# Three edits in the tail of a float32 decoder layer: where split weights lie, when a head's second products run, and how the last block is folded into the residual

## The chip, the cores and the metric

The kernel runs on one core of one Trainium2 chip. The metric is device time in microseconds (us), from the first to the last instruction with what lies around it, median of three runs. A profiled execution on the chip gives the trace that the rows below come from. Engines: TensorE (PE: matrix products), VectorE (DVE), ScalarE (ACT), GpSimd (POOL) and SyncE (SP), whose queue here issues nearly all transfers.

## The reference, cut to what matters

One decoder layer over 1024 tokens and 1024 channels in float32. Three attention branches give outputs `o_A`, `o_B`, `o_C` (1024 x 512 each); then:

```
# o_n @ P_n: branch n, 512 -> 1024 channels; G_n: its gate
x = x + (sum_n sigmoid(G_n) * (o_n @ P_n)) @ W_o  # merge and output projection
h = rms_norm(x, norm_mlp)
x = x + square(relu(h @ W_up)) @ W_down           # 1024 -> 4096 -> 1024
```

All three edits lie in these lines, the last 900 us of the kernel; attention stands before them and is not touched.

## The kernel before, in words

**Arithmetic.** Every float32 matrix product is done as three products of split parts: an operand is split into a high part `h` (ScalarE copies it to the rounded type, line 90) and a low part `l`, source minus high (line 91, on VectorE or GpSimd), and `mm3` (lines 112 to 117) adds h·h, h·l and l·h into one PSUM bank. So each weight block costs a load on SyncE's queue into a raw tile `wr`, a ScalarE copy and a subtraction. TensorE runs in the written order; the other engines' orders come from a planner that simulates the program with modelled costs and lets whatever is ready first, by program order, go first. Each engine, and each queue of transfers, then works strictly in that order. A tile pool hands a buffer on when its last reader is done.

**Merge (`merge_and_mlp`, lines 1151 to 1197).** Branch A was multiplied earlier. Branch B: eight blocks d by two halves of the tokens (`half`), each a product of 12 matmuls (`branch`) into one of six banks; VectorE multiplies it with the gate `g` (line 1179; gates are loaded through two buffers), GpSimd adds it to `y` (line 1181). Branch C: for each half, eight blocks; VectorE does the gate (1190), the addition (1192) and the low part of the result (1194), ScalarE the high part (1193), giving `mh`, `ml`, the operand of the output projection. The weights' split parts come from `weight` and `parts`: three buffers of each part, in pool `pre`. The pools `bb` (split `ob`), `br` (`y` and `oc` of half 0) lie on the right above `pre`, `bl` (`y`, `oc` of half 1) and `bg` (gates) on the left.

**Output projection (`tail`, lines 1231 to 1309).** The eight k-blocks of W_o are split into `wo`, whose first four lie where `bb` was and last four where `br` was. Each half block is loaded into one of the three raw tiles `wr` of `pre`, which the branches' weights use too, and split, with the subtraction on VectorE for odd k and on GpSimd for even k. Then come eight row tiles of 128 tokens in the order 0, 4, 1, 5, 2, 3, 6, 7: two halves of 24 matmuls into a bank each, added to `x1` (the loaded residual; tag x1, two buffers in pool `xp`, line 1298), stored to `xd`, normed (`norm`) and, one row tile later, transposed on TensorE. From row tiles 4 to 7 `operands` makes sums of blocks as well: `tt`, `rb` on VectorE (lines 1280 to 1288) and the split operands t1, t2, t3, t4.

**MLP.** Both matrix products go by Winograd's form of Strassen's scheme: 2 x 2 blocks, seven products (numbers 1 to 7) instead of eight; products 2, 7 and 3 are added in the banks of 1, 6 and 5 (`chain`), after VectorE or ScalarE has read those. Weights (and, for the down product, the stored activations) are combined in sums `s1` to `s4`, `t1` to `t4` (`sums`, line 1224). *Up stage*: 16 pairs of blocks, products in the order 1, 6, 5, 2, 7, 4, 3 (`ORDER`), 12 matmuls each. The first four pairs (`HEAD`) do products 1 and 2 early, straight from loaded weights, while row tile 7 is being transposed and split: `after(1)` copies product 1's bank to `e1` on ScalarE (line 1366), then product 2 goes on in that bank. Activations are combined and stored to `ud`. *Down stage*: eight batches `b` of two pairs. In each batch seven products in `order`; per product and pair the stored `ud` is loaded into `v` (tag v, four buffers, line 1458) and split with VectorE, the weight is loaded by `raw` (seven raw tiles over two pools, line 1329), summed on GpSimd (line 1224) and split with GpSimd. Four row tiles j of 6 matmuls follow, and VectorE adds each bank to its accumulator (line 1477): products 1, 6, 7 to `sums`, products 2 to 5 to `x1`. In the last batch `sums` are folded into `x1` after products 6 and 7 (line 1481), eight additions on VectorE and twelve on GpSimd, and each finished piece is stored.

Of the kernel before, what the change touches and what calls it, by code (L numbers as in the profile page):

```python
# [11 lines left out]
F32 = mybir.dt.float32  # L12
F32R = mybir.dt.float32r
AF = mybir.ActivationFunctionType
# [3 lines left out]
P = 128  # L18
# [57 lines left out]
class Kernel:  # L76
# [27 lines left out]
    def parts(self, pool=None, bufs=None, tag="w"):  # L104
        return [(pool or self.wp).tile([P, self.w_n], F32R, name=tag + x, tag=tag + x, bufs=bufs or self.w_bufs)
                for x in "hl"]
# [64 lines left out]
    def run(self):  # L171
# [3 lines left out]
        self.spreads = []  # L175
        self.urgent = URGENT
# [974 lines left out]
    def merge_and_mlp(self):  # L1151
# [9 lines left out]
        with (tc.tile_pool(name="bb", side="right", **kw) as bb, tc.tile_pool(name="br", side="right", **kw) as br,  # L1161
              tc.tile_pool(name="bl", side="left", **kw) as bl, tc.tile_pool(name="bg", side="left", **kw) as bg):
# [68 lines left out]
    def tail(self, mp, mh, ml, halves, pre):  # L1231
# [10 lines left out]
        for k in range(KT):  # L1242
            for s in halves:
                r = pre.tile([P, 512], F32, name="wr", tag="wr", bufs=3)
                nc.sync.dma_start(r, a["wo"][k, :, s])
                self.split(wo[k][0][:, s], wo[k][1][:, s], r, nc.vector if k % 2 else nc.gpsimd)
# [4 lines left out]
        def norm(t, x1):  # L1251
# [7 lines left out]
            def operands():  # L1259
# [28 lines left out]
                sub(b21, b21, t2)  # L1288
# [4 lines left out]
        self.first = {}  # L1293
        HEAD = 4
# [23 lines left out]
        last = {}  # L1318
# [95 lines left out]
        for i in range(1, HEAD):  # L1414
# [4 lines left out]
            pairs[i - 1].product(2, 1, True)  # L1419
        pairs[-1].product(2, 1, True)  # L1420
# [4 lines left out]
        for o in pairs:  # L1425
            up(o, [i for i in self.ORDER if i not in (1, 2)])
        for p in range(HEAD, H):
# [8 lines left out]
        into = {2: lambda j: x1[j][:, lo], 3: lambda j: x1[j][:, hi], 4: lambda j: x1[4 + j][:, lo],  # L1436
                5: lambda j: x1[4 + j][:, hi]}
        G = 2
        order = (1, 6, 7, 2, 5, 4, 3)
# [7 lines left out]
        for b in range(0, H, G):  # L1447
# [5 lines left out]
            final = b + G == H  # L1453
            for i in order:
                forms = []
                for q in range(G):
                    u = temp("v")
# [9 lines left out]
                for j in range(4):  # L1467
# [5 lines left out]
                    dst = sums[i][j] if i in sums else into[i](j)  # L1473
                    if i in sums and b == 0:
                        nc.scalar.activation(dst, ps, AF.Copy)
                    else:
                        nc.vector.tensor_tensor(dst, dst, ps, op=ALU.add)
                    if not final:
                        continue

                    add = lambda o, x, eng: eng.tensor_tensor(o, o, x, op=ALU.add)  # L1481
                    if i == 6:
                        add(sums[6][j], sums[1][j], nc.gpsimd)
# [70 lines left out]
```

## Time and profile before

| | us |
|---|---|
| median of 3 runs (lowest, highest) | 2107.08 (2104.51, 2108.21) |
| the profiled execution's own time | 2108.54 |
| its span, first to last instruction | 2106.7 |
| TensorE busy in the span | 1956.2 |
| VectorE, ScalarE, GpSimd busy in the span | 1404.5, 1020.7, 956.9 |

The profiled execution lies 1.46 us above the median of the runs and has 1.84 us around its span. Busy time is an average over stages with different limits, so the tail is read stage by stage. Stages, by TensorE: merge from 1219 us, output projection from 1313.8, up stage from 1427, down stage from 1757.5, end at 2106.7.

### The profile page before, as it was taken

The page shows a single profiled execution, that of the slowest core. Times are in us where ns is not written, and L with a number is a line of the kernel's source. Part 1 is how long each engine was busy: PE and PEld are TensorE (multiplying, and loading weights), DVE is VectorE, ACT ScalarE, POOL GpSimd, SP SyncE. Part 2 cuts the span into 40 slices and gives each one's busy share as a digit, 9 for nine tenths or more (in the row PEclk, how much of TensorE's full clock was granted, in tenths as well). Part 3 has the DMA queues.
Part 4 walks back from the last instruction along what each step waited for, and adds up shares of the span by engine and source line. Part 5 has one row for each costly group of instructions (what it writes and reads, how often), then busy time and mean ns, then how long its engine had stood idle before and what let it go on. Part 6 is the DMA issues. An engine that isn't in the chain of part 4 may idle for free. (4 is left out here: it accounts for less than half of the span.)

```text
span 2106.7 us, 30550 instructions
## 1 busy us (share of the span) xinstructions
PE 1956.2 (93%) x9806; PEld 1613.4 (77%) x9806; DVE 1404.5 (67%) x3207; ACT 1020.7 (48%) x2622; POOL 956.9 (45%) x1149
## 2 busy tenths in 40 slices
PE   6999998998799999999999799898999998999997
PEld 6778777788678778887888677686788886877876
DVE  5747667778848667647776736358645544888877
ACT  5355455566636555536565523324444544433332
POOL 4455345354252212162222145227444445878777
PEclk9999999999999999999999999899999999999998
DMA  6131012011211111202243366424444436444443
GB/s 212 49 101 49 6 54 57 13 49 35 85 27 59 60 47 53 75 28 88 80 129 99 119 224 188 132 85 156 171 143 150 150 137 222 147 144 140 141 134 110
DMA packets 122909, 218.42 MB, mean 104 GB/s; under 512 B 14260, under 2 KB 35252, under 8 KB 122748
## 3 DMA queue, kind: packets, MB, share of 16 engines
q1 hardware_dynamic: 118076, 202.84, 30.0%
q10 hardware_dynamic: 4672, 13.63, 1.8%
q8 instruction: 77, 1.26, 0.3%
q14 instruction: 84, 0.69, 0.1%
HBM read 155.54 MB, written 64.81 MB: 105 GB/s over the span
## 5 line engine op out<-in xcount | busy, mean ns | idle before, releaser
L91 POOL TENSOR_TENSOR wl<-wr,wh 128x512 fp32r<-128x512 f32 (+3 forms) x246 | 320.4, 1309 | 300.5 <-ACT wh L90 242.9
L90 ACT ACTIVATE wh<-wr 128x512 fp32r<-128x512 f32 (+3 forms) x258 | 150.4, 590 | 217.6 <-PE mm L116 130.0
L697 PE MATMUL sc<-st 128*128 128x256 f32 (+5 forms) x736 | 199.3, 352 | 16.0 <-ACT p L729 15.8
L90 ACT ACTIVATE ph<-tr 128x384 fp32r<-128x384 f32 (+3 forms) x280 | 138.3, 496 | 117.0 <-PE tr L745 98.5
L91 DVE TENSOR_TENSOR pl<-tr,ph 128x384 fp32r<-128x384 f32 (+3 forms) x280 | 155.5, 558 | 46.2 <-ACT ph L90 43.0
L742 POOL MEMSET ph<- 128x128 f32 x152 | 34.1, 224 | 304.5 <-PE ac L887 265.2
L697 PEld LDWEIGHTS sc<-st 128*128 128x128 f32 x736 | 124.8, 189 | 56.6 <-ACT p L729 24.3
L116 PE MATMUL mm<-wl,wh 128*128 128x512 f32 x352 | 142.7, 405 | 22.6 <-POOL wl L91 22.6
L115 PE MATMUL mm<-hh,wh 128*128 128x512 f32 x384 | 159.6, 416 | 0.0
L117 PE MATMUL mm<-hh,wl 128*128 128x512 f32 x384 | 152.0, 396 | 0.0
L116 PE MATMUL mm<-hl,wh 128*128 128x512 f32 x384 | 151.9, 396 | 0.0
L745 PE MATMUL tr<-ident,p 128*128 128x128 f32 x792 | 132.2, 280 | 15.4 <-ACT o L875 7.9
L91 DVE TENSOR_TENSOR wl<-v,wh 128x512 fp32r<-128x512 f32 x112 | 132.6, 1188 | 20.7 <-ACT wh L90 16.8
L115 PE MATMUL mm<-wh 128*128 128x512 f32 x352 | 140.8, 400 | 2.8 <-ACT wh L90 2.8
L117 PE MATMUL mm<-wh,wl 128*128 128x512 f32 x352 | 141.1, 401 | 0.0
L729 ACT ACTIVATE p<-sc,mc 128x256 f32<-128x256 f32 (+5 forms) x200 | 106.7, 538 | 52.3 <-DVE mc L721 50.2
L887 PE MATMUL ac<-ph,st 128*128 128x256 f32 x392 | 110.2, 299 | 19.1 <-DVE ob L894 13.0
L115 PE MATMUL mm<-wh,hh 128*128 128x384 f32 (+1 forms) x320 | 125.0, 391 | 0.0
L91 POOL TENSOR_TENSOR wl<-s,wh 128x512 fp32r<-128x512 f32 x64 | 87.0, 1363 | 81.9 <-ACT wh L90 78.8
L115 PE MATMUL mm<-mh,wh 128*128 128x512 f32 x256 | 102.5, 400 | 9.5 <-ACT e L1366 9.2
L888 PE MATMUL ac<-pl,st 128*128 128x256 f32 x392 | 105.8, 291 | 5.7 <-DVE pl L91 4.9
L745 PEld LDWEIGHTS tr<-ident,p 128*128 128x128 f32 x792 | 91.9, 142 | 24.8 <-ACT o L875 10.5
(308 smaller groups left out, 5733.5 us busy)
## 6 DMA issues: line engine op xcount, KB each, us to landing
ud<-u SPq DMA_DIRECT2D x112, 256.0 KB, 2.1
v<-ud SPq DMA_DIRECT2D x112, 256.0 KB, 2.8
wr<-wu SPq DMA_DIRECT2D x72, 256.0 KB, 2.8
wr<-wd SPq DMA_DIRECT2D x64, 256.0 KB, 2.9
gd<-go SPq DMA_DIRECT2D x48, 256.0 KB, 2.0
g<-gd SPq DMA_DIRECT2D x48, 256.0 KB, 3.0
wr<-wg SPq DMA_DIRECT2D x40, 256.0 KB, 2.7
wr<-wbr SPq DMA_DIRECT2D x40, 256.0 KB, 2.8
```

Of the source, the lines that this page charges most:

```text
L90: nc.scalar.activation(hi, src, AF.Copy)
L91: (eng or nc.vector).tensor_tensor(lo, src, hi.bitcast(F32), op=ALU.subtract)
L115: mm(out, lh, rh, start=first, stop=False, skip_group_check=more)
L116: mm(out, lh, rl, start=False, stop=False, skip_group_check=more)
L117: mm(out, ll, rh, start=False, stop=last, skip_group_check=more)
L697: self.nc.tensor.matmul(ps[:, off:off + k1 - k0], q[:, t * P:(t + 1) * P], k[:, k0:k1], start=i == 0, stop=i == 1)
L729: self.nc.scalar.activation(p, ps, AF.Exp, bias=m, scale=-1.0, accum_out=l)
L742: nc.gpsimd.memset(ph[0:rows, o:o + P].bitcast(F32), 0.0)
L745: nc.tensor.transpose(pt[0:rows, o:o + P], src, self.ident)
L887: nc.tensor.matmul(ac, v, ph, start=first, stop=False)
L888: nc.tensor.matmul(ac, v, pl, start=False, stop=last)
```

## The change

- `parts` takes a weight's high and low tile in turn from `pre` and from a new pool `wx` (as many buffers again), from the merge on.
- W_o's blocks are loaded whole (512 KB, one transfer per k) into the two x1 buffers of `xp`, not in halves into the raw tiles of `pre`.
- In the up stage's head, product 2 of the four pairs runs after product 1 of all four; before, it ran one pair behind. The transposes of row tile 7 stay behind pair 1's product 1. What VectorE does for the head pairs' other products is queued behind the last block sum of row tile 7 (`last["sum"]`).
- In the down stage the order is 1, 6, 2, 7, 5, 4, 3; from the second batch on, activations load into the 12 buffers of tag u, which the sums t1 to t4 use too, and no longer into the 4 of tag v.
- In the last batch the accumulators of the earlier batches are folded into `x1` up front, twenty additions on VectorE, and each bank is added straight to the one, two or three pieces of `x1` that it belongs to: 40 additions from banks, where there were 28.

```diff
--- before.py
+++ after.py
@@ -102,8 +102,11 @@
         return hi, lo
 
     def parts(self, pool=None, bufs=None, tag="w"):
-        return [(pool or self.wp).tile([P, self.w_n], F32R, name=tag + x, tag=tag + x, bufs=bufs or self.w_bufs)
-                for x in "hl"]
+        pool = pool or self.wp
+        if self.other is not None:
+            self.turn += 1
+            pool = self.other if self.turn % 2 else pool
+        return [pool.tile([P, self.w_n], F32R, name=tag + x, tag=tag + x, bufs=bufs or self.w_bufs) for x in "hl"]
 
     def spare(self, k):
 
@@ -173,6 +176,7 @@
         PS = bass.MemoryType.PSUM
         self.lag, self.turn = [], 0
         self.spreads = []
+        self.other = None
         self.urgent = URGENT
         self.through = True
         self.dram = tc.alloc_tile_pool(name="dram", bufs=1, space=bass.MemoryType.DRAM)
@@ -1159,7 +1163,9 @@
         self.wp = pre
         self.w_n, self.wr_bufs, self.w_bufs = 512, 3, 3
         with (tc.tile_pool(name="bb", side="right", **kw) as bb, tc.tile_pool(name="br", side="right", **kw) as br,
-              tc.tile_pool(name="bl", side="left", **kw) as bl, tc.tile_pool(name="bg", side="left", **kw) as bg):
+              tc.tile_pool(name="bl", side="left", **kw) as bl, tc.tile_pool(name="bg", side="left", **kw) as bg,
+              tc.tile_pool(name="wx", side="left", **kw) as wx):
+            self.other = wx
             ob = [[bb.tile([P, S], F32R, name=f"ob{i}{x}") for x in range(2)] for i in range(4)]
             oc = [None, None]
             y = [None, None]
@@ -1240,10 +1246,10 @@
         wps = [tc.alloc_tile_pool(name=f"wo{i}", side="right", **kw) for i in range(2)]
         wo = [[wps[k // 4].tile([P, D], F32R, name=f"wo{k}{x}") for x in range(2)] for k in range(KT)]
         for k in range(KT):
+            r = xp.tile([P, D], F32, name="x1", tag="x1", bufs=2)
+            nc.sync.dma_start(r, a["wo"][k])
             for s in halves:
-                r = pre.tile([P, 512], F32, name="wr", tag="wr", bufs=3)
-                nc.sync.dma_start(r, a["wo"][k, :, s])
-                self.split(wo[k][0][:, s], wo[k][1][:, s], r, nc.vector if k % 2 else nc.gpsimd)
+                self.split(wo[k][0][:, s], wo[k][1][:, s], r[:, s], nc.vector if k % 2 else nc.gpsimd)
         g = xp.tile([P, D], F32, name="g2")
         nc.scalar.dma_start(g, a["norm_mlp"].broadcast_to([P, D]))
 
@@ -1285,12 +1291,13 @@
                 self.split(mh[:, 0:4, ts], ml[:, 0:4, ts], wide(t1), nc.gpsimd)
                 sub(b11, t2, b11)
                 self.split(th["t3"][0][:, :, js], th["t3"][1][:, :, js], wide(b11), nc.gpsimd)
-                sub(b21, b21, t2)
+                last["sum"] = nc.vector.tensor_tensor(b21, b21, t2, op=ALU.subtract).ins
                 self.split(th["t4"][0][:, :, js], th["t4"][1][:, :, js], wide(b21))
 
             return operands
 
         self.first = {}
+        last = {}
         HEAD = 4
         late = []
         for t in (0, 4, 1, 5, 2, 3, 6, 7):
@@ -1315,7 +1322,6 @@
             moving[n] = (*th[n], 0, lo)
         main = more = None
         count = dict(f=0, r=0)
-        last = {}
 
         def form():
             count["f"] += 1
@@ -1416,14 +1422,15 @@
             pairs[i].after(1)
             if i == 1:
                 late.pop()()
-            pairs[i - 1].product(2, 1, True)
-        pairs[-1].product(2, 1, True)
+        for o in pairs:
+            o.product(2, 1, True)
         xp.release()
         more = tc.alloc_tile_pool(name="more", side="right", **kw)
         for o in pairs:
             o.after(2)
         for o in pairs:
-            up(o, [i for i in self.ORDER if i not in (1, 2)])
+            with tc.issue_after(last["sum"]):
+                up(o, [i for i in self.ORDER if i not in (1, 2)])
         for p in range(HEAD, H):
             up(up_pair(p), self.ORDER)
         tf.release()
@@ -1433,10 +1440,11 @@
         acc = tc.alloc_tile_pool(name="acc", side="left", **kw)
         x1 = [acc.tile([P, D], F32, name=f"x1{t}") for t in range(NT)]
         sums = {i: [acc.tile([P, 512], F32, name=f"a{i}{j}") for j in range(4)] for i in (1, 6, 7)}
-        into = {2: lambda j: x1[j][:, lo], 3: lambda j: x1[j][:, hi], 4: lambda j: x1[4 + j][:, lo],
-                5: lambda j: x1[4 + j][:, hi]}
+        place = {2: lambda j: (j, lo), 3: lambda j: (j, hi), 4: lambda j: (4 + j, lo), 5: lambda j: (4 + j, hi)}
+        place.update({i: place[5] for i in sums})
+        add = lambda o, x: nc.vector.tensor_tensor(o, o, x, op=ALU.add)
         G = 2
-        order = (1, 6, 7, 2, 5, 4, 3)
+        order = (1, 6, 2, 7, 5, 4, 3)
         banks = 0
 
         def bank():
@@ -1451,10 +1459,17 @@
                 gets.append(self.sums(wd, temp, "t", nc.gpsimd))
             held = {}
             final = b + G == H
+            if final:
+                for j in range(4):
+                    add(sums[6][j], sums[1][j])
+                    add(x1[j][:, hi], sums[6][j])
+                    add(sums[7][j], sums[1][j])
+                    add(x1[4 + j][:, lo], sums[7][j])
+                    add(x1[4 + j][:, hi], sums[7][j])
             for i in order:
                 forms = []
                 for q in range(G):
-                    u = temp("v")
+                    u = temp("u" if b else "v")
                     nc.sync.dma_start(u, ud[b + q][i])
                     forms.append((splitted(u, nc.vector), splitted(gets[q](self.BSIDE[i]), nc.gpsimd)))
                 if b == 0 and i in (1, 6):
@@ -1470,24 +1485,18 @@
                     for q in range(G):
                         (uh, ul), (wh, wl) = forms[q]
                         self.mm3(ps, uh[:, js], ul[:, js], wh, wl, q == 0 and not chain, q == G - 1, bool(chain))
-                    dst = sums[i][j] if i in sums else into[i](j)
-                    if i in sums and b == 0:
-                        nc.scalar.activation(dst, ps, AF.Copy)
-                    else:
-                        nc.vector.tensor_tensor(dst, dst, ps, op=ALU.add)
-                    if not final:
+                    if i in sums and not final:
+                        if b == 0:
+                            nc.scalar.activation(sums[i][j], ps, AF.Copy)
+                        else:
+                            add(sums[i][j], ps)
                         continue
 
-                    add = lambda o, x, eng: eng.tensor_tensor(o, o, x, op=ALU.add)
-                    if i == 6:
-                        add(sums[6][j], sums[1][j], nc.gpsimd)
-                        add(x1[j][:, hi], sums[6][j], nc.gpsimd)
-                    elif i == 7:
-                        add(sums[7][j], sums[1][j], nc.vector)
-                        add(x1[4 + j][:, lo], sums[7][j], nc.gpsimd)
-                        add(x1[4 + j][:, hi], sums[7][j], nc.vector)
-                    if i in into:
-                        t, s = {2: (j, lo), 3: (j, hi), 4: (4 + j, lo), 5: (4 + j, hi)}[i]
+                    t, s = place[i](j)
+                    for t, s in {1: ((j, hi), (4 + j, lo), (4 + j, hi)), 6: ((j, hi),),
+                                 7: ((4 + j, lo), (4 + j, hi))}.get(i, ((t, s),)):
+                        add(x1[t][:, s], ps)
+                    if final and i in (2, 3, 4, 5):
                         nc.sync.dma_start(a["out"][t * P:(t + 1) * P, s], x1[t][:, s])
         acc.release()
         more.release()
```

## Rows read from the trace of the kernel before

**Rows 1.** The profile page's first part: TensorE's busy time over the whole span, its share, its instructions.

```profile
PE 1956.2 (93%) x9806; PEld 1613.4 (77%) x9806; DVE 1404.5 (67%) x3207; ACT 1020.7 (48%) x2622; POOL 956.9 (45%) x1149
```

**Rows 2.** The windows view, one stretch of the tail a line: its length, then busy time (and instructions) of each engine, the granted clock, the DMA share, GB/s. Branch 1; branch 2; the first two row tiles of the output projection; its other six; the head of the up stage; the stretch after it.

```profile
1219.00:1265.60 46.60, 44.52 (x192) 35.91 (x193) 15.46 (x19) 9.26 (x15) 23.09 (x18) 1.00 0.77 257
1265.60:1313.80 48.20, 45.38 (x194) 35.50 (x193) 29.66 (x43) 17.10 (x30) 28.80 (x22) 1.00 0.58 179
1313.80:1355.20 41.40, 31.84 (x99) 20.82 (x98) 17.30 (x24) 12.62 (x21) 11.92 (x10) 0.75 0.49 158
1355.20:1427.00 71.80, 71.80 (x343) 59.57 (x342) 34.26 (x47) 19.82 (x38) 11.16 (x10) 1.00 0.23 85
1427.00:1461.70 34.70, 25.47 (x108) 20.07 (x107) 33.46 (x28) 20.68 (x38) 32.75 (x20) 0.90 0.44 147
1461.70:1520.00 58.30, 54.72 (x232) 42.88 (x231) 38.64 (x47) 25.47 (x42) 27.29 (x21) 1.00 0.52 180
```

**Rows 3.** The waits view of TensorE from 1150 us on: engine and line, whom it waited for, us in total, times, the longest.

```profile
PE mm L116 <- POOL wl L91: 22.6, 12, 4.2
PE mm L115 <- ACT e L1366: 9.2, 2, 7.6
```

**Rows 4.** The timeline of SyncE's queue around the output weights: start, length, queue, line, transfer.

```profile
1304.40 0.33 SPq L1245 DMA_DIRECT2D wr<-wo  x1
...
1318.52 14.87 SPq L1245 DMA_DIRECT2D wr<-wo  x10
```

**Rows 5.** The tile view of wo: an engine's instructions on it with their shortest, median and longest ns, first and last start; the last line is the time from issue to landing of its transfers.

```profile
L90 ACT ACTIVATE wo<-wr x16: 613/630/635, 1308.1 to 1335.7; 128x512 fp32r<-128x512 f32 x16
L91 POOL TENSOR_TENSOR wo<-wr,wo x8: 1267/1284/1787, 1308.8 to 1333.2; 128x512 fp32r<-128x512 f32 x8
DMA to landing us min/median/max: 2.5/2.9/3.7
```

**Rows 6.** The timeline of VectorE in the merge: the last lower parts of half 0 and the last of half 1.

```profile
1301.90 1.29 DVE L1194 SCALAR_TENSOR_TENSOR ml<-y,mh 128x512 fp32r<-128x512 f32 x2
...
1323.75 0.69 DVE L1194 SCALAR_TENSOR_TENSOR ml<-y,mh 128x512 fp32r<-128x512 f32 x1
```

**Rows 7.** The lines view of VectorE in the merge, 1219 to 1325 us: group and count, busy us, mean ns, idle before it and what ended it.

```profile
L1179 DVE SCALAR_TENSOR_TENSOR g<-g,mm 128x512 f32<-128x512 f32 x16 | 10.9, 685 | 32.0 <-DMA g<-gd 26.7 <-PE mm L117 5.1
```

**Rows 8.** The source view of L1299, the loads of the residual rows x1 (512 KB each): the time from issue to landing.

```profile
DMA to landing us min/median/max: 3.4/3.4/10.9
```

**Rows 9.** The timeline of ScalarE in the head: the copies e of pairs 2 and 3, and two splits between them.

```profile
1446.05 0.58 ACT L1366 ACTIVATE e<-mm 128x512 f32<-128x512 f32 x1
...
1453.92 1.15 ACT L90 ACTIVATE wh<-s 128x512 fp32r<-128x512 f32 x2 [4.40 <-DVE s L1224]
...
1456.71 0.58 ACT L1366 ACTIVATE e<-mm 128x512 f32<-128x512 f32 x1
```

**Rows 10.** The timeline of VectorE in the head: the first and the last of the eleven sums s of the head pairs before 1461.7 us.

```profile
1436.19 1.20 DVE L1224 TENSOR_TENSOR s<-wr 128x512 f32<-128x512 f32 x1
...
1460.54 1.77 DVE L1224 TENSOR_TENSOR s<-wr 128x512 f32<-128x512 f32 x1
```

**Rows 11.** The windows view of the down stage, one batch of two pairs a line (third, fourth, fifth, seventh and eighth), and last a stretch across the seventh and eighth.

```profile
1846.20:1885.20 39.00, 38.43 (x170) 31.47 (x169) 33.06 (x42) 14.80 (x27) 27.67 (x20) 1.00 0.43 138
1885.20:1927.80 42.60, 39.80 (x170) 32.51 (x169) 34.48 (x42) 16.19 (x30) 34.02 (x24) 0.96 0.44 128
1927.80:1967.50 39.70, 38.68 (x170) 31.39 (x169) 32.55 (x42) 15.38 (x29) 34.16 (x24) 1.00 0.51 162
2006.50:2051.50 45.00, 40.81 (x170) 33.24 (x169) 34.12 (x42) 15.01 (x28) 31.67 (x23) 0.92 0.42 135
2051.50:2103.70 52.20, 43.55 (x169) 34.28 (x167) 43.09 (x47) 11.84 (x21) 43.65 (x29) 0.90 0.31 107
2035.20:2090.10 54.90, 48.53 (x194) 39.06 (x193) 48.02 (x53) 17.79 (x32) 51.11 (x34) 0.91 0.29 92
```

**Rows 12.** The waits view of SyncE's queue in the down stage.

```profile
SPq L1458 <- DVE wl L91: 142.7, 61, 7.7
SPq L1329 <- POOL wl L91: 68.6, 36, 5.0
```

**Rows 13.** The timeline of GpSimd at the start of the seventh batch: a sum u, then the split wl that TensorE waits for.

```profile
2008.31 1.72 POOL L1224 TENSOR_TENSOR u<-wr,u 128x512 f32<-128x512 f32 x1
2010.00 1.70 POOL L91 TENSOR_TENSOR wl<-wr,wh 128x512 fp32r<-128x512 f32 x1
```

**Rows 14.** The lines view of VectorE from 1755 us to the end.

```profile
L91 DVE TENSOR_TENSOR wl<-v,wh 128x512 fp32r<-128x512 f32 x108 | 129.8, 1206 | 15.4 <-ACT wh L90 11.4 <-POOL u L1224 3.6
L1477 DVE TENSOR_TENSOR x<-x,mm 128x512 f32<-128x512 f32 x112 | 75.6, 680 | 18.4 <-PE mm L117 17.5
L1481 DVE TENSOR_TENSOR a<-a,a 128x512 f32<-128x512 f32 x4 | 7.0, 1762 | 0.0
L1481 DVE TENSOR_TENSOR x<-x,a 128x512 f32<-128x512 f32 x4 | 4.7, 1174 | 0.0
L1224 DVE TENSOR_TENSOR u<-u 128x512 f32<-128x512 f32 x4 | 2.6, 688 | 1.9 <-ACT u L1389 1.8
```

**Rows 15.** The same view of GpSimd.

```profile
L1481 POOL TENSOR_TENSOR x<-x,a 128x512 f32<-128x512 f32 x8 | 13.7, 1728 | 0.0
L1481 POOL TENSOR_TENSOR a<-a,a 128x512 f32<-128x512 f32 x4 | 5.5, 1399 | 0.0
```

## The prediction

> **What bounds the kernel now.** I began with the profile page: TensorE is busy for 93% of the span [rows 1], so a change can pay only where it stands still or runs slowly. The tail alone is touched, so the windows view came next, cut at its stages [rows 2]. The six later row tiles of the projection are the measure of health: 71.8 us with no idle time, 11.97 us a tile. The first two take 41.4 us, 31.84 busy, at a granted clock of 0.75: partly the lower of its two levels (1.2 of 2.4 GHz), after waits. The two branches idle for 2.1 and 2.8 us, the up stage's head for 9.2 of 34.7 us. Third, TensorE's waits: GpSimd's low parts of weights lead, then two waits for ScalarE's copy e [rows 3]. Then the down stage batch by batch [rows 11]: the healthy ones take 39.0 us, the others up to 52.2. The reader is to see four separate leaks: W_o's arrival, the head, the batch borders, and the last batch.
>
> **Part 1: split parts in two pools, W_o through the x1 buffers.** The loads of W_o start at 1304.40 and the last ten hold the queue until 1333 [rows 4], since they share three raw tiles with the branch weights. A 256 KB load lands after 2.9 us, ScalarE needs 0.63, GpSimd 1.28 [rows 5]: 4.8 us per turn of three tiles, 1.6 each, 26 us for sixteen. TensorE reached W_o at 1313.8 and paid 41.4 - 2 x 11.97 = **17.5 us**. After the change the loads need no raw tile. The first four blocks need only `bb`, free when branch 1's products end at 1265.6; the last four need `br`, free when half 0's last low part is done, at 1301.90 + 1.29 = 1303.2 [rows 6]. Two x1 buffers turn slowly: a 512 KB load landed in 3.4 us at best [rows 8], plus two copies of 0.63 and two subtractions of 1.28, 7.2 us for two blocks. So blocks 4 and 5 are split by about 1307 and 6 and 7 by about 1314, and row tile 0 needs the last one some 5 us after it starts. The residual's own load for tile 0, made early so far, must now follow block 6's split; it has the first 24 matmuls (about 5.6 us) as cover, and without it would hold a bank, not TensorE.
> More buffers for split parts let ScalarE and GpSimd run further ahead, which takes away some of the branches' 4.9 us of idle; the gate loads remain, for which VectorE waited 26.7 us in branch 1 [rows 7], and they are late next: row tile 4 needs all of half 1, whose last low part ended at 1323.75 + 0.69 = 1324.4 [rows 6]. Row tile 0 fills the time until then, row tile 4 ends near 1324 + 12 = 1336, where it ended at 1355.2. I take **-20 us**. Ends: -22.4 (both losses vanish), and -12 if the added work on SyncE's queue moves the merge's end by 8 us. Each load waits there for the split two blocks before it, and the gates queue behind it.
>
> **Part 2: the head.** Eight products of 12 matmuls, each a quarter of a 48-matmul row tile (2.8 us), and one tile's transposes (0.8) make 23.2 us; the stretch took 34.7, so **11.5** are lost. Pair 2's and 3's copies e ran at 1446.05 and 1456.71, the latter behind splits that waited for VectorE's sums s [rows 9], eleven of which stood among row tile 7's own [rows 10]. Now the products 1 end by about 1439, the copies have some 5 us or more before products 2 want the banks, and the sums stay behind row tile 7's last. Nothing else on the new order costs TensorE anything: both early products read operands of the first half alone. But the sums moved back must be made later: eight of them, at up to 1.77 us, 14 us on VectorE, which has 58.3 - 38.64 = 19.7 us free in the next stretch [rows 2], in pieces. The next products 6 and 7 then wait for sums. I take 3 us back: **-8 us**, ends -11.5 and 0.
>
> **Part 3: order and buffers of the down stage.** Over the 39.0 us of a healthy batch, the fourth, fifth and seventh take 3.6, 0.7 and 6.0 us more [rows 11], **10.3** in all; the third is the healthy one, and the second and sixth, which have no row, are counted as healthy too. SyncE's queue stood 142.7 us at loads of v for VectorE to free one of four buffers, with weight loads queued behind; but also 68.6 us at weight loads for raw tiles, which the change leaves alone [rows 12]. In the seventh batch GpSimd made a sum just ahead of the split that TensorE stood still for [rows 13]. Product 2 has no sum of its own, so ahead of product 7 it gives GpSimd one product's time; twelve buffers, some held by sums, let loads run further ahead. No new instruction is issued here. One cause of two eased: **-5 us**, ends -10.3 and +2 (sums kept out of u by early loads). The first batch keeps its four buffers v and its place behind the up stage's stores, so its losses are taken to stay.
>
> **Part 4: the last batch.** It took 52.2 us, 13.2 over a healthy one [rows 11]. GpSimd loses its twelve folds, 13.7 + 5.5 = 19.2 us [rows 15], which stood among its splits. VectorE loses eight, 7.0 + 4.7 = 11.7 us [rows 14]. It gains twelve additions from banks at 0.68, 8.2 us, and twenty folds: 20 x 0.688 = 13.8 us at the length of an addition in SBUF without company, or 8 x 1.76 + 12 x 1.17 = 28.1 at the lengths of today's folds [rows 14]. Net +10.3 to +24.6 us. From 2035.2 to 2090.1 VectorE has 54.9 - 48.02 = 6.9 us idle [rows 11]. So it becomes the bound: +3.4 to +17.7 us by that account. Against it: with GpSimd emptier, the splits shorten from 1.21 towards 0.69 (ten remaining ones: up to 5 us), the 13.2 us that TensorE lost can partly be used, and nothing on TensorE waits for a fold until product 2 wants the banks of product 1, two products (11 us) in. I take **+2 us**, nearer the company-free end because GpSimd's load halves there; ends -8 and +18.
> One rule speaks against reading a bank three times: the Trainium skill, "VectorE: DVE Perf Modes", Rules for kernel authors, offers copying it to SBUF first where many operations follow. Here the trace says otherwise, 0.68 us from a bank [rows 14] against 1.17 from SBUF beside GpSimd.
>
> **Sum.** -20 - 8 - 5 + 2 = -31 us. Against the profiled execution's 2108.5 this gives 2077.5; that lies 1.46 above the median, so I forecast **2076 us**.
>
> **Rivals.**
> *The folds are as slow as today's and VectorE bounds the last batch.* For: today's folds all ran beside GpSimd [rows 14]. Against: GpSimd has less to do. Price: +18 in place of +2, 2092 us. The Trainium skill, "SBUF — State Buffer", Who interferes with whom, says that a VectorE instruction with two inputs in SBUF and a GpSimd one that reads SBUF exclude each other for a whole instruction, while one such input is free of this. The trace agrees (0.68 and 1.17 to 1.76); by it alone, every fold would meet the case.
> *The gates' chain takes part 1's gain.* VectorE's idle time for gates [rows 7] grows as the queue gets W_o's waits. Price: -8 in place of -20, 2088 us.
> *The head's gain comes back as waits for the late sums.* Price: 0 in place of -8, 2084 us.
> *The queue stands still (slower than before).* SyncE's queue is strict: if the planner places loads 2 to 7 of W_o ahead of the gates, each holds them for a turn, 3.4 + 1.26 + 2.56 = 7.2 us, 43 in all. It decides only when the merge's end moves by more than 31 us, the whole gain. With all 43 the time is 2076 + 43 = 2119 us. Against: the planner issues a load where its own simulation finds the buffer free.
> *It does not do what it says in the tail of the down stage.* If sums keep their place and folds cost what they did, parts 3 and 4 are 0: 2079, within the forecast.
>
> **Chances.** The forecast with its own bounds (2064 to 2086), 0.55; better than that, parts 3 and 4 near their good ends, 0.11; slow folds 0.14; gates 0.07; the head 0.05; queue 0.04; several misses that cancel out near 2107, 0.04. The range, 2060 to 2098, leaves out about 2 in 10. The three runs before spread by 3.7 us, so about 0.2% (4 us) can be told from no change: faster 0.92, same 0.04, slower 0.04.
>
> **What would show it.** Right: loads of W_o before 1300, row tiles 0 and 4 back to back at a granted clock of 1.00, ending near 1336; both copies e well before their products 2, no wait of TensorE at them; head about 8 us shorter; GpSimd no longer the releaser in the last batch, VectorE nearly without idle time there, at about 50 us. Wrong: gate loads later than before and TensorE idle at row tile 4 beyond 1330; the waits in the head now on sums; a last batch over 60 us with VectorE's additions as releasers, folds of 1.2 us and more.

## The result and the profile after

The changed kernel takes 2087.3 us, median of four runs (2083.9 to 2093.3); the kernel before, on the same chip, 2105.8 (2104.1 to 2108.2). The ratio is **0.9914** [0.9888, 0.9941]: 18.5 us faster, where 31 were forecast; 2087.3 lies in the range. The profiled execution is the slowest of the four (2093.3, span 2091.5), so its stages add up to 6 us more than the median.

The windows view after, cut at the same places as [rows 2], with the stretch ahead of the merge in front and the whole up stage at the end:

```profile
1153.90:1224.00 70.10, 56.86 (x297) 47.10 (x295) 51.09 (x146) 37.41 (x100) 16.32 (x31) 0.90 0.39 124
1224.00:1271.00 47.00, 45.15 (x192) 35.54 (x193) 14.01 (x19) 9.38 (x15) 21.76 (x18) 1.00 0.78 259
1271.00:1322.90 51.90, 46.78 (x194) 36.86 (x194) 32.63 (x41) 20.16 (x35) 34.50 (x25) 0.97 0.60 188
1322.90:1351.00 28.10, 25.81 (x99) 19.96 (x98) 17.21 (x26) 7.21 (x12) 4.18 (x4) 0.88 0.46 158
1351.00:1422.30 71.30, 71.30 (x338) 59.08 (x337) 33.80 (x47) 19.83 (x38) 11.16 (x10) 1.00 0.23 83
1422.30:1446.20 23.90, 23.90 (x112) 19.55 (x111) 23.63 (x21) 14.11 (x26) 21.51 (x14) 1.00 0.48 151
1446.20:1754.70 308.50, 295.11 (x1249) 236.21 (x1248) 159.89 (x204) 148.30 (x245) 141.99 (x106) 0.98 0.45 151
```

The two stretches that [rows 2] does not have, in the kernel before:

```profile
1152.40:1219.00 66.60, 53.98 (x297) 44.54 (x295) 48.79 (x146) 35.79 (x97) 12.13 (x28) 0.95 0.37 119
1461.70:1757.50 295.80, 292.22 (x1249) 234.23 (x1248) 151.23 (x197) 141.18 (x232) 131.80 (x101) 1.00 0.44 152
```

W_o's loads, behind the branches' in [rows 4], now begin in branch 1; the first and the last on SyncE's queue:

```profile
1232.04 1.45 SPq L1250 DMA_DIRECT2D x<-wo  x2
...
1321.62 2.58 SPq L1250 DMA_DIRECT2D x<-wo  x2
```

The reader is to see two gains that are given back. Row tiles 0 and 4 take 28.1 us in place of 41.4, but the three stretches before them are 3.5, 0.4 and 3.7 us longer: 5.7 of 13.3 are left. The head has no idle time any more (23.9 us, all busy); before, the same work took 35.2, from 1426.5 to 1461.7 ([rows 2] begins at 1427.0). But the up stage behind it is 12.7 us longer. Where, the waits view of TensorE from 1150 us on says (compare [rows 3]):

```profile
PE mm L118 <- DVE u L1375: 11.8, 4, 8.6
PE mm L118 <- DVE x L1445: 10.2, 4, 4.1
...
PE mm L119 <- POOL wl L91: 5.8, 4, 3.4
PE mm L118 <- DVE g L1185: 5.4, 4, 3.5
```

GpSimd's splits no longer lead (22.6 us before), nor the copies e (9.2): four waits are for VectorE's addition u (product 6's bank), four for its additions x in the last batch. VectorE's timeline from the head into the up stage shows the first:

```profile
1436.00 1.78 DVE L1230 TENSOR_TENSOR s<-wr 128x512 f32<-128x512 f32 x1
...
1458.80 1.02 DVE L1230 TENSOR_TENSOR s<-wr,s 128x512 f32<-128x512 f32 x1 [0.66 <-DMA wr<-wu]
1459.74 0.68 DVE L1375 TENSOR_TENSOR u<-mm,e 128x512 f32<-128x512 f32 x1
```

Pair 0's product 6 ended at 1449.2 and product 5 behind it at 1452.0. Product 7 came next; it is added in product 6's bank, and the addition u that reads this bank first stood behind sums s, most of 1.6 to 1.8 us, for pairs that were not due yet. TensorE waited 8.56 us, until 1460.56.

In row tiles 0 and 4 TensorE's waits, 2.3 us in all, are for the splits of W_o's last two blocks, in row tile 0; 3.6 us more went to the matmuls behind them, which ran at the lower clock level for a while (0.88 on average in the windows view). The reason stands in ScalarE's timeline: the copies of blocks 4 and 5, whose place the pool `br` holds until half 0's last lower part is made, began when VectorE had made it, at 1317.5, and only their splits freed the x1 buffers for the last two loads (1321.62). TensorE's waits from 1320 to 1352 us, then ScalarE's line:

```profile
PE mm L118 <- ACT wo L90: 1.1, 1, 1.1
PE mm L119 <- POOL wo L91: 0.6, 1, 0.6
PE mm L119 <- DVE wo L91: 0.6, 1, 0.6
```

```profile
1317.56 2.20 ACT L90 ACTIVATE wo<-x 128x512 fp32r<-128x512 f32 x4 [1.10 <-DVE ml L1200]
```

Half 1's last lower part, made at 1340.3, held nothing up: row tile 4 began at 1339.8, needed that part only for its last k-block, at 1344.6, and ran without a wait.

The down stage by windows, as in [rows 11]: fourth, seventh and last batch.

```profile
1879.40:1917.50 38.10, 38.10 (x170) 31.56 (x169) 35.46 (x45) 16.07 (x30) 34.70 (x24) 1.00 0.49 157
...
1994.80:2034.70 39.90, 39.11 (x169) 31.12 (x167) 37.99 (x43) 14.96 (x27) 34.98 (x23) 1.00 0.43 142
2034.70:2087.50 52.80, 42.61 (x168) 33.27 (x168) 47.92 (x71) 11.82 (x21) 25.98 (x17) 0.94 0.30 105
```

42.6, 45.0 and 52.2 us became 38.1, 39.9 and 52.8. A batch without a stall is 38.1 us, not 39.0. From its first product to the end the down stage is 12.4 us shorter, most of the 15.2 us by which the span fell.

### The profile page after: what moved, and what is told of

Read it like the earlier page. It is cut to its first block, busy times and chain, and to the rows that moved or that the text cites. A ratio compares the mean times of both kernels' runs of the same rounds, so it can differ in the third digit from the quotient of the medians.

```text
span 2091.5 us, 30581 instructions
## 1 busy us (share of the span) xinstructions
PE 1953.5 (93%) x9806; PEld 1614.9 (77%) x9806; DVE 1414.6 (68%) x3231; ACT 1019.6 (49%) x2622; POOL 946.5 (45%) x1137
## 5 line engine op out<-in xcount | busy, mean ns | idle before, releaser
L91 POOL TENSOR_TENSOR wl<-wr,wh 128x512 fp32r<-128x512 f32 (+3 forms) x246 | 324.6, 1326 | 317.7 <-ACT wh L90 261.7
L701 PE MATMUL sc<-st 128*128 128x256 f32 (+5 forms) x736 | 201.5, 356 | 14.5 <-ACT p L733 14.3
L118 PE MATMUL mm<-wh 128*128 128x512 f32 x352 | 140.0, 398 | 12.9 <-DVE x L1445 10.2
L90 ACT ACTIVATE wh<-u 128x512 fp32r<-128x512 f32 x162 | 93.0, 620 | 106.2 <-PE mm L119 27.3
L91 DVE TENSOR_TENSOR wl<-u,wh 128x512 fp32r<-128x512 f32 x98 | 111.4, 1138 | 1.8 <-ACT wh L90 1.8
L749 PEld LDWEIGHTS tr<-ident,p 128*128 128x128 f32 x792 | 92.4, 142 | 24.9 <-ACT o L879 10.7
```

The lines of the kernel that those rows point to most:

```text
L90: nc.scalar.activation(hi, src, AF.Copy)
L91: (eng or nc.vector).tensor_tensor(lo, src, hi.bitcast(F32), op=ALU.subtract)
L118: mm(out, lh, rh, start=first, stop=False, skip_group_check=more)
L701: self.nc.tensor.matmul(ps[:, off:off + k1 - k0], q[:, t * P:(t + 1) * P], k[:, k0:k1], start=i == 0, stop=i == 1)
L749: nc.tensor.transpose(pt[0:rows, o:o + P], src, self.ident)
```

## The experiments

All ratios are against the kernel before, run on the same chip. The windows of every experiment are cut at the same instructions.

**1. Each part alone.** The edits are the hunks of the change for that part; the key line of each:

```diff
 p1_weights:  +            pool = self.other if self.turn % 2 else pool
              +            r = xp.tile([P, D], F32, name="x1", tag="x1", bufs=2)
 p2_head:     +        for o in pairs:
              +            o.product(2, 1, True)
              +            with tc.issue_after(last["sum"]):
 p3_down:     +        order = (1, 6, 2, 7, 5, 4, 3)
              +                    u = temp("u" if b else "v")
 p4_folds:    +            if final:
              +                for j in range(4):
              +                    add(sums[6][j], sums[1][j])
```

> Part 1 alone (split parts in two pools, W_o through the x1 buffers). Theory read from the changed kernel's trace: the gates' chain in the merge ends about 11 us later and takes back much of what W_o's early arrival gives; from the merge's start to the up stage's start the stretch shrinks by some 9 us (208 to 199), and up to 4 us come back before it, so 2097 to 2101 us. Rival, as predicted: row tiles 0 and 4 are done 20 us earlier and the time is 2086 to 2089 us.

> Part 2 alone (products 2 of the head behind all products 1, the head pairs' VectorE work behind row tile 7's last sum). Theory: the waits for the copies e vanish, product 6 of pair 0 starts 11 us earlier, and a wait of 8 to 9 us for VectorE's addition of its bank, queued behind sums, gives it back: no change, 2104 to 2109 us. Rival, as predicted: 8 us faster, 2096 to 2099 us.

> Part 3 alone (order 1, 6, 2, 7 and the 12 buffers u). Theory: it removes nearly all waits at the borders of the second to seventh batch, 13 to 14 us, and some of the last batch's: 2088 to 2093 us. Rival, as predicted: half of 10 us, 2100 to 2102 us.

> Part 4 alone (folds up front on VectorE, banks straight into x1). Theory: VectorE takes GpSimd's place as the releaser in the last batch and it costs 0 to 4 us: 2106 to 2110 us. Rival (folds as slow as today's and nothing given back): 16 us or more lost, 2122 us. Second rival (GpSimd's folds were the whole loss): 8 us gained, 2098 us.

Measured: part 1 0.9979 [0.9966, 0.9992], 2100.2 us; part 2 1.0009 [0.9997, 1.0022], 2109.3; part 3 0.9916 [0.9900, 0.9932], 2087.7; part 4 1.0041 [1.0025, 1.0057], 2114.9. In us of 2106: -4.4, +1.9 (not clear of no change), -17.7, +8.6. **Part 3 alone brings as much as the whole change.** With part 3 alone GpSimd's splits still hold TensorE up in the down stage, for 13.0 us; with part 4 alone VectorE's bank additions do, 10.7 us in one wait. That one stands at product 7, which is added in the bank of product 6, in the old order directly behind it; part 3's order puts product 2 between the two. TensorE's waits in those two kernels, part 3's from 1750 us and part 4's in its last batch:

```profile
PE mm L116 <- POOL wl L91: 13.0, 7, 3.5
```

```profile
PE mm L115 <- DVE x L1438: 15.2, 3, 10.7
```

**2. The head: the bank addition first.**

```diff
+                    last["u2"] = nc.vector.tensor_tensor(o.u2, o.ps[6], o.e1, op=ALU.add).ins
...
-            with tc.issue_after(last["sum"]):
+            with tc.issue_after(last.get("u2", last["sum"])):
```

> The changed kernel with one edit: in the head, the sums of pairs 1 to 3 stand on VectorE behind the addition that empties the bank of the pair before (product 6), not ahead of it. Theory: the head's gain of 11.3 us is given back because that addition of pair 0 stood behind sums of the other pairs (TensorE waited 8.56 us for it at 1452.00). Then that wait shrinks to under 1 us, the sums come later where TensorE does not need them at once, and the time falls by 5 to 8 us against the changed kernel's 2087.3: 2079 to 2082. Rival (VectorE simply has too little time for the late sums): TensorE's wait moves to splits that wait for the sums of pairs 1 to 3, and the time stays within 2 us of 2087. Forecast on record: the head gains 8 us of 11.5; it says nothing of this order.

Measured 0.9902 [0.9884, 0.9921], 2084.5 us: too near the changed kernel for the times to decide, but the trace does. The wait of 8.56 us is gone, and one of nearly its size stands at the first pair behind the head, whose sums were not held back. TensorE's waits from 1440 to 1720 us:

```profile
PE mm L118 <- DVE u L1375: 7.8, 1, 7.8
PE mm L118 <- ACT wh L90: 1.8, 1, 1.8
```

**3. Part 1 in two halves.** W_o through the x1 buffers only, then two pools only:

```diff
 p1x_wo_by_x1:   +            r = xp.tile([P, D], F32, name="x1", tag="x1", bufs=2)
                 +            nc.sync.dma_start(r, a["wo"][k])
 p1w_two_pools:  +            self.other = wx
```

> The kernel before with half of part 1: W_o is loaded through the x1 buffers, the split parts stay in one pool of three. Theory A (the loss in the stretch ahead of the merge comes from the additional buffers, whose splits run earlier; the loss in branch 2 comes from W_o's splits among the branch's own work): the stretch ahead of the merge is 66 to 68 us as before, branch 2 takes 50 to 53 us instead of 48.2, row tiles 0 and 4 take 27 to 32 us instead of 41.4; sum -4 to -9 us, 2097 to 2102. Theory B (both losses come from the load queue): the stretch ahead of the merge is 70 us or more here too, and the time is 2099 to 2103. Forecast on record: this half carries nearly all of the 20 us, 2086 to 2090.

> The kernel before with the other half of part 1: the split parts alternate between two pools of three, W_o goes through the old raw tiles. Theory A: ScalarE and GpSimd make six instead of three pairs of the merge's split parts ahead of 1219 us, beside attention's last work, and the stretch from attention's last products to the merge grows from 66.6 to 70 to 74 us; row tiles 0 and 4 stay at 38 to 42 us; time +2 to +6 us, 2108 to 2112. Theory B (that stretch is longer for another reason): it stays at 66 to 68 us, and the time is 2104 to 2107. Forecast on record: a small gain, 0 to -5 us, from the branches' idle time.

Measured: 0.9969 [0.9956, 0.9983], 2099.7 us, and 0.9981 [0.9969, 0.9993], 2101.7. Each half gains, and together they gain no more than one. Of the forecasts on record the first half's (2086 to 2090) failed, the second's (0 to -5 us) held. The windows (stretch ahead of the merge, branch 1, branch 2, row tiles 0 and 4) of the first and of the second:

```profile
1150.90:1219.80 68.90, 57.25 (x298) 47.41 (x297) 49.05 (x146) 35.71 (x97) 12.46 (x28) 0.90 0.36 115
...
1267.40:1322.40 55.00, 46.88 (x193) 36.66 (x192) 35.92 (x42) 21.69 (x38) 37.40 (x27) 0.97 0.61 194
1322.40:1347.20 24.80, 22.75 (x99) 18.07 (x98) 17.86 (x25) 7.47 (x13) 5.26 (x4) 1.00 0.53 182
```

```profile
1148.60:1223.40 74.80, 60.87 (x298) 50.22 (x296) 51.28 (x146) 36.99 (x100) 16.83 (x31) 0.84 0.37 116
1223.40:1267.20 43.80, 43.80 (x192) 36.14 (x193) 14.72 (x19) 9.38 (x15) 23.17 (x18) 1.00 0.83 280
1267.20:1311.30 44.10, 44.10 (x194) 36.09 (x193) 30.69 (x39) 16.09 (x27) 26.22 (x21) 1.00 0.61 185
1311.30:1348.10 36.80, 28.08 (x99) 19.44 (x98) 20.39 (x28) 11.84 (x20) 10.56 (x8) 0.81 0.49 162
```

Two pools take all idle time out of both branches: 43.8 and 44.1 us, all busy. W_o's early loads take most of it out of row tiles 0 and 4 (24.8, of which 2.1 idle) and put 6.8 us into branch 2 (55.0 against 48.2, and above theory A's 50 to 53). So branch 2 pays for W_o's early route; whether by its loads (theory B) or its splits (A) the two do not tell. Theory A's first half falls: with two pools alone the stretch ahead of the merge is longer (74.8), but its idle time is 74.80 - 60.87 = 13.9 us against 12.6 before; TensorE is busy longer, at a granted clock of 0.84. Theory A's time, 2108 to 2112, fell too.

**4. W_o's lower parts all on VectorE.**

```diff
-                self.split(wo[k][0][:, s], wo[k][1][:, s], r[:, s], nc.vector if k % 2 else nc.gpsimd)
+                self.split(wo[k][0][:, s], wo[k][1][:, s], r[:, s], nc.vector)
```

> The changed kernel with one edit: all lower parts of W_o are made by VectorE, half of them were GpSimd's. Theory: in branch 1's end and branch 2 GpSimd's splits of W_o (eight of 1.27 to 1.75 us, four of them between 1274.8 and 1286) stood among the branch's own additions and splits and held up the gates' buffers; without them TensorE's wait of 3.55 us at 1282.2 goes, half 1's last lower part ends 4 to 8 us earlier than 1340.3, and the time falls by 3 to 6 us against 2087.3: 2081 to 2084. Rival 1 (the gates' own loads stand in the queue behind W_o's loads): no change, 2086 to 2089. Rival 2 (VectorE, which makes the gates' products, is the late one): slower, 2089 to 2095.

Measured 0.9900 [0.9883, 0.9917], 2085.2 us: between theory and rival 1, undecided. Branch 2 took 49.3 us and row tiles 0 and 4 26.6, but half 1's last lower part still ended 16.9 us after branch 2's last product (17.4 in the changed kernel): the lag is not GpSimd's. TensorE's waits for W_o's last blocks in row tile 0 stayed too, 2.0 us against 2.3. The stretch ahead of the merge was 66.4 us, at 0.95, with both pools in place: one more mark against the first half of experiment 3's theory A.

**5. Four gate buffers.**

```diff
+            bufs = 2 if self.turn % 2 else bufs
...
-                    g = self.gate(bg, "g", 2, 1, d, s)
+                    g = self.gate(bg, "g", 4, 1, d, s)
```

(branch 2's line likewise).

> The changed kernel with four gate buffers in place of two; their 4 KB come from the second pool of split parts, which holds two pairs in place of three. Theory (the gates' chain holds part 1's gain: a gate is loaded only after the addition y that frees one of two buffers, so half 1's last lower part ends 17.4 us after branch 2's last product, where 10.6 us were needed before): gates are loaded ahead, the last lower part ends 9 to 13 us after branch 2's last product, branch 2 takes 47 to 49 us in place of 51.9, row tiles 0 and 4 take 24 to 26 us in place of 28.1; the time falls by 4 to 8 us against 2087.3: 2079 to 2083. Rival (the load queue itself, or VectorE's own splits of W_o among the gates' work, is what is late): under 2 us of change, 2085 to 2089.

Measured 0.9884 [0.9865, 0.9903], 2079.0 us. The interval overlaps the changed kernel's, so the trace has to say whether the cure works. The windows of branch 2 and of row tiles 0 and 4:

```profile
1262.70:1313.20 50.50, 46.44 (x193) 37.00 (x192) 41.38 (x43) 22.70 (x41) 39.50 (x26) 0.97 0.71 224
1313.20:1335.40 22.20, 22.20 (x99) 18.14 (x98) 14.34 (x20) 5.22 (x9) 4.65 (x4) 1.00 0.39 131
```

Row tiles 0 and 4 run without idle time, and the lag fell from 17.4 to 12.0 us. That lag, half 1's, was the wrong place to look, since TensorE never waited for it. What counts is half 0's last lower part, which lets W_o's blocks 4 to 7 in: it ended 5.4 us before branch 2's last product in the changed kernel and 13.2 us before it here, and the last two loads of W_o went at 1305.53, 7.7 us before row tile 0, where it was 1.3. ScalarE's copies of blocks 4 and 5, and the last loads:

```profile
1300.04 2.20 ACT L90 ACTIVATE wo<-x 128x512 fp32r<-128x512 f32 x4 [0.56 <-DVE ml L1201]
```

```profile
1305.53 1.66 SPq L1251 DMA_DIRECT2D x<-wo  x2
```

What moved half 0's part is in VectorE's lines view of the merge, branch 2's gate product in the changed kernel and here (busy us, mean ns, idle before it):

```profile
L1196 DVE SCALAR_TENSOR_TENSOR g<-g,mm 128x512 f32<-128x512 f32 x16 | 10.9, 683 | 11.3 <-DMA g<-gd 11.2
```

```profile
L1197 DVE SCALAR_TENSOR_TENSOR g<-g,mm 128x512 f32<-128x512 f32 x16 | 10.8, 676 | 0.0
```

So **the gates' chain held part 1's gain in row tiles 0 and 4**, by way of half 0's last lower part and W_o's last blocks. Branch 2 missed its 47 to 49 us: TensorE waits there for GpSimd's splits now, 4.1 us in three.

**6. Without part 4, and with mixed folds.** The first edit is part 4's hunk taken back, the second:

```diff
-        add = lambda o, x: nc.vector.tensor_tensor(o, o, x, op=ALU.add)
+        add = lambda o, x, eng=nc.vector: eng.tensor_tensor(o, o, x, op=ALU.add)
...
-                    add(sums[6][j], sums[1][j])
-                    add(x1[j][:, hi], sums[6][j])
+                    add(sums[6][j], sums[1][j], nc.gpsimd)
+                    add(x1[j][:, hi], sums[6][j], nc.gpsimd)
```

> The changed kernel without part 4: parts 1, 2 and 3, the last batch folded as before. Theory (part 4 costs 3 to 5 us on top of part 3, since the last batch took 48.6 us with part 3 alone and 52.8 with all four): the time falls by 3 to 5 us against 2087.3, 2082 to 2085. Rival A (the parts do not add up because part 4 alone cost 9 us and costs as much here): 2077 to 2080. Rival B (the folds at the batch's start and the ones between are worth the same once part 3 has relieved GpSimd): 2086 to 2089. Forecast on record: part 4 costs 2 us.

> The changed kernel with eight of the last batch's twenty folds (those of product 6 and of the upper halves of tiles 0 to 3) on GpSimd, which is busy for 24 of that batch's 55 us; VectorE keeps twelve and all additions from banks. Theory (TensorE's four waits in the last batch, 10.2 us, are for banks that VectorE empties late because twenty folds stand ahead of its additions): VectorE is free about 10 us earlier, those waits shrink to 2 to 5 us, and the time falls by 3 to 7 us against 2087.3: 2080 to 2084. Rival (GpSimd's folds stand ahead of its splits and its company makes VectorE's folds slow): TensorE waits for GpSimd's splits instead, the time stays at 2086 to 2091.

Measured 0.9909 [0.9892, 0.9926], 2085.6 us, and 0.9905 [0.9886, 0.9923], 2084.4. Neither can be told from the changed kernel, 0.9914. Part 4 costs 8.6 us alone and nothing measurable behind parts 1 to 3: rival A fell, and 2085.6 lies between the theory's range and rival B's, nearer to rival B's. In the traces it trades one wait for another: without it TensorE waits 5.8 us for GpSimd's splits in the last batch, with it 10.2 for banks, with mixed folds 5.4 for banks and 1.3 for a split.

**7. Three cures at once.** Experiments 5 and 6's mixed folds, and experiment 2's order for all sixteen pairs:

```diff
         for p in range(HEAD, H):
-            up(up_pair(p), self.ORDER)
+            with tc.issue_after(last["u2"]):
+                up(up_pair(p), self.ORDER)
```

> The changed kernel with three cures at once: four gate buffers (second pool of split parts two pairs), eight of the last batch's folds on GpSimd, and the sums of every pair of the up stage, not of pairs 1 to 3 alone, behind the product 6 bank addition of the pair before. Theory: the first two gave 8.3 and 2.9 us each against 2087.3 and lie in different stages, so they add up to 11; the third gave 2.8 us with a wait of 7.8 us left at the first pair behind the head, at 1493.4, where the sums were not held back: with that wait gone too it gives 6 to 10. Together 2066 to 2071. Rival A (that wait only moves on to a later pair, as the first one did): the third cure keeps its 2.8 us, 2072 to 2076. Rival B (sums of all pairs bound to their place make TensorE wait for splits throughout the up stage): the stretch from the head to the down stage is longer than the changed kernel's 308.5 us and the time is over 2078.

Measured **0.9777** [0.9763, 0.9790], **2060.0 us**: 27 us under the changed kernel, 6 better than the best bound. Branch 2, row tiles 0 and 4, and the up stage in the windows view:

```profile
1263.40:1311.10 47.70, 45.07 (x193) 35.61 (x192) 42.03 (x43) 22.12 (x40) 35.02 (x23) 1.00 0.69 218
1311.10:1333.30 22.20, 22.20 (x99) 18.15 (x98) 14.35 (x20) 5.23 (x9) 4.66 (x4) 1.00 0.39 131
1428.60:1720.00 291.40, 291.40 (x1249) 234.28 (x1248) 138.87 (x204) 144.17 (x245) 140.31 (x106) 1.00 0.47 160
```

The up stage has no idle time at all: 308.5 became 291.4 us, 17.1 from the order of the sums, where 6 to 10 were expected. VectorE does the same 204 instructions in 138.9 us in place of 159.9. Two rows of each lines view show how, the changed kernel first:

```profile
L1230 DVE TENSOR_TENSOR u<-u 128x512 f32<-128x512 f32 x60 | 54.3, 944 | 19.6 <-ACT u L1395 19.1
L1230 DVE TENSOR_TENSOR s<-wr 128x512 f32<-128x512 f32 x30 | 27.0, 899 | 44.8 <-POOL wl L91 39.4 <-DMA wr<-wu 5.4
```

```profile
L1231 DVE TENSOR_TENSOR u<-u 128x512 f32<-128x512 f32 x60 | 39.2, 693 | 20.9 <-ACT u L1396 20.4
L1231 DVE TENSOR_TENSOR s<-wr 128x512 f32<-128x512 f32 x30 | 21.5, 716 | 0.0
```

## Why the prediction was right and where it was wrong

The time fell into the range because errors of both signs partly cancelled, not because the terms were right; it lies 1 us outside the forecast's own bounds (2064 to 2086), and the range was wide enough for that. Alone, the parts measured -4.4, +1.9, -17.7 and +8.6 us; forecast were -20, -8, -5 and +2. In the changed kernel's trace, the stretches from the one ahead of the merge to row tile 4 gave 5.7 us where 20 were forecast, the head and the up stage lost 1.4 where 8 were to be gained, and the down stage gave 12.4 where parts 3 and 4 were to give 3.

**Part 1 (forecast -20).** The leak was named rightly: the first six loads of W_o came early, row tiles 0 and 4 became 13.3 us shorter, and 19.2 with four gate buffers (22.2 us, experiment 5). The step that failed took the merge's own times as fixed: half 0's last lower part at 1303.2, so W_o's last blocks split by about 1314, and "row tile 4 ends near 1336". Half 0's part ended at 1317.5, the last blocks were split at 1331.8, and row tile 4 ended at 1351.0: 9.1 us because the projection began later (5.0 for the merge's later start, 4.1 for longer branches) and 5.9 because row tile 0 had to wait for W_o after all. With the part alone, row tiles 0 and 4 gave 14.8 us; branch 2 took back 4.8 and the stretch ahead of the merge, for which the prediction had no price, 6.7, at a granted clock of 0.86. Whether part 1 causes that last loss is open. The rival "the gates' chain takes part 1's gain" was given 0.07 and a price of 12 us, against 15.6 missed when the part ran alone. Its cause was half right: VectorE waited for the gates, but not only since "the queue gets W_o's waits": a gate could be loaded only into one of two buffers, and two more cured it with W_o's loads still on the same queue. The gain expected from more split buffers was real, and bigger than taken, when nothing else came with it: both branches ran without idle time, 6.9 us shorter together (experiment 3).

**Part 2 (forecast -8).** The first half of the reasoning held: the copies e are early, the first at 1427.35 and the last at 1441.77, and the head lost its 11.3 us. The step that failed is "I take 3 us back". All of it came back, 12.7 us; the rival "the head's gain comes back as waits for the late sums" (0.05) is what happened, with one correction: TensorE waited not for a late sum but for a bank addition *behind* early ones. The step priced VectorE's total free time (19.7 us), while what mattered was the order: one 0.68 us instruction that frees a bank, queued behind work that nobody needed yet.

**Part 3 (forecast -5, ends -10.3 and +2).** Right in direction, too small in size, beyond its own better end: -17.7. The step that failed is the halving, "one cause of two eased": with part 3 alone the fourth, fifth and seventh batches gained 11.0 us, more than the 10.3 counted there. Two assumptions failed beside it. A batch of 39.0 us was called healthy, but 38.1 is; and the first, second, third and sixth batches, counted at nothing, gained 3.9, the last one 3.0: 48.5 us with part 3 alone, counted up to the last product, against 51.5. SyncE's waits at the loads of stored activations [rows 12] fell from 142.7 us, all for VectorE's splits, to 99.5 in the changed kernel, of which 34.0 for those; its waits at raw weights for GpSimd's splits rose from 68.6 to 99.2. Whether the order or the buffers did it was not separated.

**Part 4 (forecast +2, ends -8 and +18).** Alone +8.6, behind the other parts nothing measurable (0.9914 against 0.9909): the forecast's +2 holds for the whole change. The folds measured 1.22 us (a<-a,a, 1.76 before) and 1.12 us (x<-x,a, 1.17 before), 23.2 us in all, where the prediction's two cases were 13.8 and 28.1; so "the folds are slow" was half true. The wait came at the other end: the prediction said that nothing waits for a fold until product 2 wants banks, but the folds stand in the queue ahead of the additions that free banks, and TensorE waited 7.6 us in product 1 already.

**The queue** did not stand still: SyncE waited at W_o's loads for 8.8 us in all between 1224 and 1330, not 43, and the rival of 2119 us lost.

The prediction weighed VectorE's slow additions beside GpSimd for the folds alone. They bore on the sums of the head more, where the same addition took 1.78 us in the crowd and 0.68 in its place. The Trainium skill, "SBUF — State Buffer", Who interferes with whom, says that a VectorE instruction with two inputs in SBUF contends with a GpSimd one that reads SBUF; the trace agrees (1.78 and 0.68 us).

## What to carry to other kernels

A gain at one place was kept here only where the next instruction that frees a bank or a buffer did not stand behind early work in its engine's queue: read, for each engine, what stands ahead of the instructions that release TensorE, not how much free time it has. Where a planner puts ready work first, bind that work to a place behind the release; here two such lines were worth 17 us in the up stage. Before pricing a chain's end as fixed, look for its smallest pool: two gate buffers held back the last blocks of W_o, whose loads had been set free. And look up what TensorE waits for before blaming the tile that is made last: the late lower part of half 1 cost nothing, that of half 0 did.

## What the runs showed of the hardware that was not expected

The stretch ahead of the merge, on the same 297 or 298 products, took from 66.4 to 74.8 us, with idle time of 11.7 to 14.5 in all kernels: the rest goes with the granted clock, from 0.95 (66.4, 66.5, 66.6 us) over 0.90 (68.9, 70.1) to 0.84 (74.8). What sets it is open. The kernels without part 1 all lie at 66.6 to 67.6 us, those with part 1 or half of it at both ends (0.84 and 0.95); each kernel has one trace, so a difference between executions is not ruled out.

The same VectorE addition with two SBUF inputs took 0.69 us wherever GpSimd ran nothing beside it: 97 of the 121 sums in the up stage's trace of experiment 7, 68 of 121 in the changed kernel. Where GpSimd ran all the while it took 1.60 us on average in the changed kernel (ten sums, 1.02 to 1.78) and 1.78 in experiment 7 (four). The order alone moved 29 sums out of GpSimd's company, and GpSimd's own busy time stayed (140.3 against 142.0 us).
